# A Strassen-split decoder block on one core: operand pairs for nine Strassen steps per unit, steps prepared in another order, smaller DMA scratch

## The chip, the cores and the metric

The kernel runs on one core of a Trainium2 chip as one program. The metric is the device time of one execution in microseconds; a time of a kernel is the median of several runs. The engines are named as in the profile: PE (TensorE matmul), PEld (its weight load), DVE (VectorE), ACT (ScalarE), POOL (GpSimd) and SP (SyncE, which here only issues loads).

## The reference

A decoder block for 256 tokens of width 4096 in float32. Nearly all of the work is three groups of dense products with 256 rows: the input projection (4096 to 20480 columns), the branch projections (2048 to 4096, twice) and the output projection (4096 to 4096).

```python
def reference(x, norm_w, w_in, pool_w, pool_scale, conv_w, conv_b, gate_b, w_branch, w_out, final_norm_w):
    b, s, d = x.shape
    for l in range(DEPTH):
        h = rmsnorm(x, norm_w[l])
        proj = jnp.einsum('bsd,de->bse', h, w_in[l])
        u_p, z_p, u_c, b_c, c_c, z_c, g_logit = jnp.split(proj, SPLIT_POINTS, axis=-1)
        y_pool = causal_multiscale_pool(u_p, pool_w[l], pool_scale[l]) * jax.nn.silu(z_p)
        y_conv = causal_gated_shortconv(u_c, b_c, c_c, conv_w[l], conv_b[l]) * jax.nn.silu(z_c)
        ys = jnp.stack([y_pool, y_conv], axis=2)
        br = jnp.einsum('bsnc,ncd->bsnd', ys, w_branch[l])
        gates = jax.nn.sigmoid(g_logit.reshape(b, s, N_BRANCHES, d) + gate_b[l])
        merged = jnp.sum(gates * br, axis=2)
        x = x + jnp.einsum('bsd,de->bse', merged, w_out[l])
    return rmsnorm(x, final_norm_w)
```

## The kernel before

**Units and steps.** The columns of every projection are cut into units of 1024. A unit adds up its products over the inner dimension in steps of 256 (two blocks of 128): 16 steps for the input and output units, 8 for the branch units. There are 20 input units (cu, cc, cz, cb for the convolution and pz, pu for the pooling, two of each; eight gate units g0_0 to g1_3), eight branch units b0_0 to b1_3, and four output units o0 to o3, in that order. All their steps together are 448 weight steps, each with 1 MB of weights. Steps of kind B and M, put into the units behind pu0 and pu1, are the pooling's own products.

**Splitting.** Each float32 factor is split into a high and a low part, and a product is three matmuls: high by high, high by low, low by high. ACT copies the high part (a rounded copy), DVE subtracts it from the factor for the low part.

**P and S steps.** A P step (plain) multiplies a 256 x 256 piece of the activations with a 256 x 1024 piece of weights as 2 x 2 x 2 blocks: 8 products, 24 matmuls of 128 x 512, into the four PSUM banks "sums". An S step does the same by a Strassen scheme with seven products, 21 matmuls, into three of these and four banks "shared", which a unit joins with four additions near its end. For that the weights' sums are needed: DVE forms two sums into the tile V, two more in place of the raw weights, and all are split like the rest. The activations' sums (Q3, Q5, Q6, Q7) are stored beside the split operand: an operand of kind P takes 4 KB per partition in the tile `arena`, one of kind S takes 7 (or 9 for the first NB of them, which can also serve as P). There are NP_X = 9 and NS_X = 7 of them; a ninth operand, LATE, is used as S in a few units with its sums kept in DRAM (late_d) and fetched into spare places.

**Which step is S.** Each unit gets a list of kinds: `spread_sequence`, `late_sequence` or `at_places`, which names the places of the S steps outright.

**Preparing.** SP loads weights into `raw`, three buffers in turn; the load of step i + 3 is issued when step i is prepared. A step's preparation is a list of small actions ("micros") with a size and a guard: the size is taken from `ring`, a ring buffer of RING KB per partition that holds split weights, and given back by the matmuls that read it. `pump`, called after every group of matmuls, writes out as many micros as ring, guard and a lookahead of AHEAD = 3 steps allow. This fixes the order of the instructions on every engine; each engine then works in order and waits on semaphores. For an S step the micros are, in this order, `sums` (V), `direct` (ACT's copy of the three direct blocks, 1536 elements, then on DVE a 512 addition, the 1536 subtraction, a 512 addition), `t13` (copy and subtraction of V, 1024) and `t24` (copy and subtraction of the two sums formed in place, 1024).

**Fills and epilogues.** Work beside the main loop is put on a queue, one item per tick; a tick is TICK = 6 matmuls. The first unit's preparation also forms the Strassen sums of x (`x_sums`, `x_parts`, at the steps listed in `seconds`). Sums across tokens' tiles are added by accumulating DMAs from POOL (`move_add`).

Of the kernel before, what the change touches and what calls it, by code (L numbers as in the profile page):

```python
# [26 lines left out]
F32 = mybir.dt.float32  # L27
# [15 lines left out]
NP_X, NS_X = 9, 7  # L43
NB = 1
NP_Y, NS_Y = (6, 5), (2, 3)
RING = 60
# [10 lines left out]
def hybrid_block(ctx: ExitStack, tc: tile.TileContext, x, x_t, norm_t, w_first, w_in, pool_w, pool_scale,  # L57
# [70 lines left out]
    late_d = dram.tile([P, 5, P], F32, name="late_d")  # L128
# [62 lines left out]
    class Operand:  # L191


        def __init__(self, kind, view, region):
            self.kind, self.view, self.region = kind, view, region
            self.ready = False
            self.more = None
            self.more_ready = False

        def block(self, part, i):  # L200

            if self.kind == "S":
                return self.view[:, part, i]
            if i in self.more:
                return self.more[i][:, part]
            return self.view[:, part, {A12: 0, A22: 0, A11: 1, A21: 1}[i], i in (A22, A21)]
# [32 lines left out]

    rg = Ring(RING)  # L240

# [5 lines left out]
    class Step:  # L247
# [7 lines left out]
        def micros(self):  # L255
# [27 lines left out]
            if self.kind == "P":  # L283
                self.blocks, self.h, self.l = [None] * 2, [None] * 2, [None] * 2
                return self.pre + [(8, None, half(0)), (8, None, half(1))] + self.post
            if self.kind == "S":
                q = r.rearrange("p (i n) -> p i n", i=4)
                tv = V

                def sums(_):  # L290
                    add(tv, q[:, 0:1].to_broadcast([P, 2, NH]), q[:, 1:3])

                def direct(block):
# [15 lines left out]
                def t24(block):  # L309
                    self.b24 = block  # L310
                    t = piece(block, 0, 8).rearrange("p (i a n) -> p i a n", i=2, a=2)
                    self.h24, self.l24 = t[:, :, 0], t[:, :, 1]
                    act(self.h24, q[:, 0:2])
                    sub(self.l24, q[:, 0:2], self.h24.bitcast(F32))

                return self.pre + self.post + [(0, None, sums), (12, None, direct), (8, None, t13), (8, None, t24)]
            if self.kind == "B":
                def parts(block):
# [4 lines left out]
                    sub(self.l, R, self.h.bitcast(F32))  # L323

                return [(16, lambda: self.unit.flags.get("base"), parts)]
            if self.kind == "M":
# [4 lines left out]
                def weights(block):  # L331
# [5 lines left out]
                    sub(self.l, q, self.h.bitcast(F32))  # L337

# [265 lines left out]
    LAST_FIRST = ('cc0',)  # L604
    SPREAD = {"cc1":(8,1),"cb1":(8,2),"cu1":{4,5,7,9,10,12,13,15},"cb0":(8,2),"cz0":(7,5),"pz0":{5,7,8,10,11,13,15},"pu0":(7,),"cz1":(7,5),"g1_3":(6,0),"pz1":(7,),"g0_0":(7,),"pu1":{4,6,8,10,12,13,15},"cc0":{2,4,6,8,10,13,15}}
# [26 lines left out]
    def in_unit(name, col, epi, seq=None, **kw):  # L632
        def src(i):
            return win[col // NU, i]
        if name in SPREAD:
            at = SPREAD[name]
            seq = at_places(at) if isinstance(at, set) else spread_sequence(*at)
# [5 lines left out]
        units.append(Unit(name, src, seq or seq_late, x_ops, epi, scaled=True, **kw))  # L643
# [3 lines left out]
    def conv_units(c, first=False):  # L647
# [32 lines left out]
        in_unit(f"cu{c}", base, lambda u: [], seq=seq_0 if first else spread_sequence(NS_X, 4), dst=Y)  # L680
        in_unit(f"cc{c}", base + 2 * HALF, c_epi, seq=seq_even if c else None)
        in_unit(f"cz{c}", base + 3 * HALF, z_epi)
        in_unit(f"cb{c}", base + HALF, b_epi, seq=seq_even)


    def pool_units(c):
# [5 lines left out]
        in_unit(f"pz{c}", HALF + c * NU, z_epi, seq=None if c else seq_turned)  # L692
# [4 lines left out]
    def make_bands(c):  # L697
        nonlocal sa, Y
        if c == 0:
            x_ops[LATE].more_ready = False  # L700

# [78 lines left out]
    def gate_unit(n, c, before=None):  # L780
# [7 lines left out]
        seq = {(0, 0): seq_late, (1, 3): spread_sequence(few)}.get((n, c), seq_even)  # L788
        if (n, c) in ((0,1),(1,1),(0,2),(1,2),(0,3),(1,0),):
            seq = spread_sequence(NS_X + 1, 1 if c else 2)  # L790
# [27 lines left out]

    def out_unit(c):
# [14 lines left out]
        seq = seq_even if c else seq_late  # L834
        if c in (2,):
            seq = spread_sequence(NS_X + 1)
        if c == 1:
            seq = at_places({2,4,6,7,9,11,13,15})

            late_s = [i for k, i in seq if k == 'S']  # L840
            late_s = iter(late_s[1:] + late_s[:1])
            seq = [(k, next(late_s) if k == 'S' else i) for k, i in seq]
        if c == 3:

            seq = spread_sequence(NS_X, 1, TAIL + 0)
        if c == 2:
            seq = at_places({2,4,6,7,9,11,13,15})
# [133 lines left out]
    def insert(u, c, owner):  # L981
# [6 lines left out]
        rest = psteps[5:]  # L988
        while ssteps:
            seq.append(ssteps.pop(0))  # L990
            if rest:
                seq.append(rest.pop(0))
        seq += rest
# [132 lines left out]
    LATE = NP_X - 1  # L1126

    def late_sums():
        o = x_ops[LATE]
        h, l = (o.view[:, part].bitcast(F32) for part in range(2))  # L1130
        q = sa[:, 4:8].rearrange("p (k t) c -> p k t c", t=2)
        add(q, h, l)
        q = q.rearrange("p k t c -> p k (t c)")
        mul(q, q, rbc[:, None].to_broadcast([P, 2, T]))
        sums_s(sa, [sa[:, i] for i in range(4, 8)])
        mul(sa[:, Q3], sa[:, Q3], std)
        move(late_d[:, 0:4], sa[:, 0:4])
        move(late_d[:, 4], sa[:, A11])

    def late_place(pool, o, blocks):  # L1140
        n = len(blocks)
# [433 lines left out]
```

## Time and profile before

| | |
|---|---|
| median of 3 runs | 2378.24 us (2378.23 to 2379.2) |
| profiled execution, first to last instruction | 2376.6 us |
| PE busy | 2364.3 us, 99% |
| DVE busy | 2170.1 us, 91% |
| ACT busy | 1392.8 us, 59% |
| POOL busy | 86.0 us, 4% |
| mean granted TensorE clock | 0.999 |
| 16 DMA engines, mean | 232 GB/s |
| weight loads, issue to landing (w_in) | 4.9 us median |

Busy times of an engine are unions: where two instructions overlap, the time counts once, so a group's busy time can be less than its count times its mean. A matmul's own 390 ns overlaps its neighbours'. An instruction's name "ring<-raw,ring 128x1024" says that it writes the tile ring from raw and ring, 128 partitions by 1024 elements. "L72 DVE" is the helper through which every two-operand vector instruction goes, so line numbers tell little and tile names tell more.

### The profile page before, as it was taken

How to read it: one execution, taken by the hardware profiler on the slowest of the kernel's cores; microseconds unless marked ns; L12 is line 12 of the kernel's file. 1: busy time of each engine (PE TensorE's matmuls, PEld its weight loads, DVE VectorE, ACT ScalarE, POOL GpSimd, SP SyncE). 2: the span in 40 equal slices, each digit the busy share in tenths (PEclk: the TensorE clock that was granted, in tenths of full speed). 3: DMA queues.
4: the chain of work that ended last, by engine and by line, in shares of the span. 5: the costliest groups of instructions: out<-in, count | busy, mean ns of one | idle time of the engine just before them, and what ended most of it. 6: DMA issues, size and time to landing. Idle time of an engine off the chain costs nothing.

```text
span 2376.6 us, 27878 instructions
## 1 busy us (share of the span) xinstructions
PE 2364.3 (99%) x10540; PEld 1957.5 (82%) x10540; DVE 2170.1 (91%) x2195; ACT 1392.8 (59%) x1452; POOL 86.0 (4%) x153
## 2 busy tenths in 40 slices
PE   9999999999999999999999999999999999999998
PEld 7888888888888888888888888888888888888886
DVE  8999999989989978979999999999898898799998
ACT  7565665656546555556655656556664556566554
POOL 0000000000010010000000000000100001000000
PEclk9999999999999999999999999999999999999999
DMA  8464665655665646655776667667766667567666
GB/s 337 161 238 170 235 251 211 217 211 213 212 239 217 238 183 221 231 200 201 259 247 214 235 237 235 228 238 260 263 249 230 226 250 289 209 214 265 241 240 264
DMA packets 83559, 551.25 MB, mean 232 GB/s; under 512 B 9616, under 2 KB 9872, under 8 KB 22240
## 3 DMA queue, kind: packets, MB, share of 16 engines
q1 hardware_dynamic: 68800, 484.51, 54.7%
q0 software_dynamic: 14192, 63.90, 9.6%
q8 instruction: 82, 1.34, 0.2%
q10 hardware_dynamic: 432, 1.07, 0.1%
q14 instruction: 53, 0.43, 0.1%
HBM read 516.60 MB, written 25.49 MB: 228 GB/s over the span
## 4 chain that ended last, share of the span: by engine, by line
PE 98%; DVE 1%; DMA 1%; ACT 0%; SPq 0%; issue 0%; DVEq 0%; ACTq 0%
PE sums L1283 74%; PE shared L1283 21%; PE shared L766 1%; PE shared L509 1%; DMA raw<-in_w_in_dram 0%; DVE R L72 0%; DVE ring L72 0%; DMA raw<-in_w_out_dram 0%; ACT ring L69 0%; PE shared L745 0%; SPq L87 0%; PE shared L746 0%; PE shared L748 0%; SPq L162 0%; ACT V L69 0%
## 5 line engine op out<-in xcount | busy, mean ns | idle before, releaser
L1283 PE MATMUL sums<-ring,arena 128*128 128x512 f32 x7890 | 1858.2, 390 | 0.5 <-ACT arena L69 0.4
L1283 PEld LDWEIGHTS sums<-ring,arena 128*128 128x128 f32 x7890 | 1478.3, 188 | 307.8 <-ACT ring L69 1.2
L69 ACT ACTIVATE ring<-raw 128x1024 fp32r<-128x1024 f32 (+2 forms) x902 | 997.5, 1145 | 703.9 <-DVE raw L72 297.3
L72 DVE TENSOR_TENSOR ring<-raw,ring 128x1024 fp32r<-128x1024 f32 (+2 forms) x902 | 1176.5, 1335 | 142.5 <-ACT ring L69 108.6
L1283 PE MATMUL shared<-ring,arena 128*128 128x512 f32 x2118 | 535.2, 389 | 0.0
L1283 PEld LDWEIGHTS shared<-ring,arena 128*128 128x128 f32 x2118 | 397.6, 188 | 82.5
L69 ACT ACTIVATE ring<-V 128x1024 fp32r<-128x1024 f32 x188 | 198.8, 1058 | 148.3 <-DVE V L72 112.7
L72 DVE TENSOR_TENSOR V<-raw 128x1024 f32<-128x1024 f32 x188 | 229.3, 1220 | 4.7 <-DMA raw<-in_w_in_dram 2.6
L72 DVE TENSOR_TENSOR ring<-V,ring 128x1024 fp32r<-128x1024 f32 x188 | 229.3, 1220 | 0.5 <-ACT ring L69 0.5
L72 DVE TENSOR_TENSOR raw<-raw 128x512 f32<-128x512 f32 x188 | 130.2, 693 | 6.5
L72 DVE TENSOR_TENSOR raw<-V,raw 128x512 f32<-128x512 f32 x188 | 130.0, 692 | 5.8
L72 DVE TENSOR_TENSOR R<-R,E 128x1024 f32<-128x1024 f32 (+1 forms) x49 | 77.5, 1591 | 1.6 <-ACT E L69 0.9
L72 DVE TENSOR_TENSOR R<-R,shared 128x512 f32<-128x512 f32 x87 | 59.5, 684 | 8.9 <-ACT R L69 5.0
L69 ACT ACTIVATE E<-sums,rin 128x512 f32<-128x512 f32 x76 | 50.0, 685 | 15.7 <-PE sums L1283 15.7
L69 ACT ACTIVATE arena<-sa 128x512 fp32r<-128x512 f32 (+2 forms) x42 | 22.4, 559 | 35.5 <-DVE sa L72 35.5
L1283 PE MATMUL shared<-ring,sums 128*128 128x512 f32 x138 | 35.9, 396 | 0.0
L1283 PEld LDWEIGHTS shared<-ring,sums 128*128 128x128 f32 x138 | 25.9, 188 | 6.0
L94 POOL DMA_DIRECT2D R<-E x8 | 7.2, 980 | 513.6 <-ACT ring L69 337.9
L69 ACT ACTIVATE E<-sums 128x512 f32<-128x512 f32 x40 | 22.2, 592 | 5.4 <-PE sums L1283 5.1
L72 DVE TENSOR_TENSOR arena<-sa,arena 128x512 fp32r<-128x512 f32 (+2 forms) x42 | 24.4, 606 | 0.7 <-ACT arena L69 0.7
L94 POOL DMA_DIRECT2D R<-in_gate_b_dram x9 | 10.1, 1119 | 356.0 <-DVE R L72 348.3
L509 PEld LDWEIGHTS shared<-ident,R 128*128 128x128 f32 x160 | 19.4, 140 | 4.2
(149 smaller groups left out, 515.8 us busy)
## 6 DMA issues: line engine op xcount, KB each, us to landing
raw<-in_w_in_dram SPq DMA_DIRECT2D x318, 1024.0 KB, 4.9
raw<-in_w_branch_dram SPq DMA_DIRECT2D x64, 1024.0 KB, 5.4
raw<-in_w_out_dram SPq DMA_DIRECT2D x64, 1024.0 KB, 5.0
gates_d<-R POOLq DMA_DIRECT2D x8, 1024.0 KB, 9.1
R<-in_gate_b_dram POOLq DMA_DIRECT2D x7, 1024.0 KB, 11.2
R<-E POOLq DMA_DIRECT2D x4, 1024.0 KB, 8.7
raw<-in_pool_w_dram SPq DMA_DIRECT2D x4, 1024.0 KB, 5.0
Y<-gates_d POOLq DMA_DIRECT2D x4, 1024.0 KB, 7.9
```

The lines of the kernel that those rows point to most:

```text
L69: return pin(nc.scalar.activation(dst, src, func, **kw))
L72: return pin(nc.vector.tensor_tensor(out=dst, in0=a, in1=b, op=op))
L94: return pin(nc.gpsimd.dma_start(dst, src, accum_op=ALU.add))
L509: pin(nc.tensor.transpose(shared(j)[:, i * T + t * P:i * T + (t + 1) * P], src[:, t, c:c + P], ident))
L766: pin(nc.tensor.matmul(o, a[:, k, ts], b[:, k], start=(k, i) == (0, 0), stop=(k, i) == (3, 2)))
L1283: pin(nc.tensor.matmul(ps, lhs, rhs, start=n == 0, stop=n == u.total[b] - 1))
```

## The change

Four things are changed together.

1. The scratch that is set aside for dynamic DMAs goes from its default, 16384 bytes per partition, to 4096. The 12 KB go to the arena (NP_X, NS_X = 7, 9 and NB = 2: 95 KB for 87) and to the ring (64 KB for 60).
2. With nine stored S operands, the operand LATE with its DRAM copy, its fetches and its spare tiles is gone; two more pairs get their sums in the first units (`seconds`).
3. The S steps' places are written out for each unit: 210 of the 448 steps are S, for 188.
4. The preparation's order: an S step begins with `direct`, which now only issues ACT's copy; then the sums into V, what is held from the step before (`settle`), the 1536 subtraction, and the first 512 addition; `t13`; a place for `t24`; then the head of the next step (its first micro, by `head_of_next`), and only then the second 512 addition and ACT's copy for `t24`. Its subtraction, `low24`, is held and is written out by the next step's `settle`, after that step's first DVE instruction; the raw buffer counts as read only then. P steps put each half's copy and subtraction in separate micros.

```diff
-NP_X, NS_X = 9, 7
-NB = 1
+NP_X, NS_X = 7, 9
+NB = 2
-RING = 60
+RING = 64
...
+    held = []
+
+    def settle():
+
+        while held:
+            held.pop(0)()
...
             if self.kind == "P":
                 self.blocks, self.h, self.l = [None] * 2, [None] * 2, [None] * 2
-                return self.pre + [(8, None, half(0)), (8, None, half(1))] + self.post
+                if self in steps[:2]:
+                    return self.pre + [(8, None, half(0)), (8, None, half(1))] + self.post
...
+                def low(n):
+                    def f(_):
+                        sub(self.l[n], q[:, :, n * NH:(n + 1) * NH], self.h[n].bitcast(F32))
+                        settle()
+                    return f
+                return self.pre + [(8, None, high(0)), (0, None, low(0)), (8, None, high(1)), (0, None, low(1))] + self.post
             if self.kind == "S":
                 q = r.rearrange("p (i n) -> p i n", i=4)
                 tv = V
-
-                def sums(_):
-                    add(tv, q[:, 0:1].to_broadcast([P, 2, NH]), q[:, 1:3])
 
                 def direct(block):
                     self.bd = block
                     d = piece(block, 0, 12).rearrange("p (i a n) -> p i a n", i=3, a=2)
                     self.dh, self.dl = d[:, :, 0], d[:, :, 1]
                     act(self.dh, q[:, 1:4])
+
+                def sums(_):
+                    add(tv, q[:, 0:1].to_broadcast([P, 2, NH]), q[:, 1:3])
+                    settle()
+                    sub(self.dl, q[:, 1:4], self.dh.bitcast(F32))
                     add(q[:, 0], tv[:, 0], q[:, 2])
-                    sub(self.dl, q[:, 1:4], self.dh.bitcast(F32))
-                    add(q[:, 1], q[:, 0], q[:, 3])
...
-                def t24(block):
+                def place24(block):
...
+                def t24(_):
+                    add(q[:, 1], q[:, 0], q[:, 3])
                     act(self.h24, q[:, 0:2])
-                    sub(self.l24, q[:, 0:2], self.h24.bitcast(F32))
-
-                return self.pre + self.post + [(0, None, sums), (12, None, direct), (8, None, t13), (8, None, t24)]
+
+                    def low24():
+                        sub(self.l24, q[:, 0:2], self.h24.bitcast(F32))
+                        self.prepared = True
+                    held.append(low24)
+
+                return self.pre + self.post + [(12, None, direct), (0, None, sums), (8, None, t13), (8, None, place24),
+                                               (0, lambda: head_of_next(self), t24)]
...
+    PLACES = {
+        "cc0": (2, 4, 6, 8, 10, 13, 15),
+        "cz0": (5, 7, 8, 10, 11, 13, 15),
+        "cb0": (3, 5, 6, 8, 9, 11, 12, 14, 15),
+        "cu1": (4, 5, 7, 9, 10, 12, 13, 14, 15),
...
+    GATE = (2, 4, 5, 7, 8, 10, 11, 13, 15)
...
+    OUT = ((5, 7, 8, 10, 11, 13, 15), (2, 4, 6, 7, 9, 11, 12, 13, 15), (2, 4, 6, 7, 9, 11, 13, 15),
+           (1, 3, 4, 6, 7, 9, 10, 12))
...
-    seconds = {14: 10, 15: 11, 16: 12, 17: 13, 19: 14, 21: 15, 28: 9}
+    seconds = {14: 10, 15: 11, 16: 12, 17: 13, 19: 14, 21: 15, 28: 9, 32: 8, 36: 7}
...
-    before(23, late_sums)
-    before(40, early_place)
-    before(41, lambda: early[0]())
-    before(42, lambda: early[1]())
...
+    def head_of_next(s):
+
+        i = state["np"] + 1
+        if i == len(steps):
+            return True
+        t = steps[i]
+        if t.kind not in "PS" or t.pre or t.post and t.kind == "S" or t.started:
+            return True
+        if i <= state["limit"] and t.raw is not None:
+            t.started = micro(t)
+        return t.started or state["np"] <= state["now"] + 1
...
-    nc = _bacc.Bacc("TRN2", target_bir_lowering=False, num_devices=1)
+    nc = _bacc.Bacc("TRN2", target_bir_lowering=False, num_devices=1,
+                     dynamic_dma_scratch_size=4096)
```

More of the change, by code (lines that the diff above doesn't have):

```diff
@@ L603, in hybrid_block @@
     few = NS_X - NB
-    LAST_FIRST = ('cc0',)
-    SPREAD = {"cc1":(8,1),"cb1":(8,2),"cu1":{4,5,7,9,10,12,13,15},"cb0":(8,2),"cz0":(7,5),"pz0":{5,7,8,10,11,13,15},"pu0":(7,),"cz1":(7,5),"g1_3":(6,0),"pz1":(7,),"g0_0":(7,),"pu1":{4,6,8,10,12,13,15},"cc0":{2,4,6,8,10,13,15}}
+    LAST_FIRST = ("cc0",)
+    PLACES = {
[13 rows of a table added]
+    }
+    GATE = (2, 4, 5, 7, 8, 10, 11, 13, 15)
     def late_sequence(ns_):
@@ L833, in src @@
             return wout[c, i]
[L834 to L847, printed above, removed]
+        seq = at_places(OUT[c])
         units.append(Unit(f"o{c}", src, seq, m_ops, epi, before=start))
```

132 lines of the change are left out of this document (48 added, 84 removed), and 9 rows, old and new, of the table PLACES.

## The prediction

> **What bounds the kernel now.** I read the page's engine shares first, then PE's groups, then everything PE ever waited for.
>
> ```profile
> span 2376.6 us, 27878 instructions
> PE 2364.3 (99%) x10540; PEld 1957.5 (82%) x10540; DVE 2170.1 (91%) x2195; ACT 1392.8 (59%) x1452; POOL 86.0 (4%) x153
> PEclk9999999999999999999999999999999999999999
> L1283 PE MATMUL sums<-ring,arena 128*128 128x512 f32 x7890 | 1858.2, 390 | 0.5 <-ACT arena L69 0.4
> L1283 PE MATMUL shared<-ring,arena 128*128 128x512 f32 x2118 | 535.2, 389 | 0.0
> ```
>
> ```profile
> PE shared L1034 <- DVE rout L1039: 1.1, 1, 1.1
> PE sums L1283 <- ACT arena L69: 0.4, 1, 0.4
> ```
>
> PE is busy for 2364.3 of 2376.6 us at the full granted clock, and the second fence is all it waited for: 1.5 us, both at the opening. From the opening to the tail the kernel is one unbroken row of matmuls, and what shortens it is fewer matmuls. What one costs is not its 390 ns, because they overlap; it is their spacing, from the chain of waits (start, length, what):
>
> ```profile
> 1277.36 11.56 PE sums L1283 x51
> 1303.35 6.12 PE sums L1283 x27
> 1359.11 11.56 PE sums L1283 x51
> ```
>
> 27 matmuls in 6.12 us is 0.2267 us each. The first and last of these lines stand at the same place of two neighbouring gate units: a unit of eight S and eight P steps takes 81.75 us. An S step is 7 products of 3 matmuls, 21 x 0.2267 = 4.76 us; a P step is 24, 5.44 us; 8 x 4.76 + 8 x 5.44 = 81.6, so a unit is its steps and next to nothing else.
>
> The second engine is DVE, 91%. It splits weights into high and low parts and forms the S sums. The stretches below are (start:end, length, then PE, PEld, DVE, ACT, POOL): units cu1, a gate unit, and o1.
>
> ```profile
> 342.10:425.70 83.60, 83.60 (x378) 69.17 (x377) 81.35 (x76) 48.03 (x47) 2.01 (x3) 1.00 0.62 225
> 1277.36:1359.11 81.75, 81.75 (x361) 67.60 (x361) 75.78 (x71) 48.48 (x47) 1.77 (x2) 1.00 0.68 232
> 2119.80:2201.50 81.70, 81.70 (x362) 67.58 (x361) 79.03 (x78) 50.68 (x52) 5.15 (x7) 1.00 0.77 264
> ```
>
> DVE has 2.25, 5.97 and 2.67 us left in them. This is the number on which the change turns.
>
> **The change on PE.** The step lists hold 188 S steps of 448 now, and 210 afterwards (91 in the input units for 81, 70 in the gates for 61, 17 in the branches as before, 32 in the output units for 29). Each of 22 steps drops 24 - 21 = 3 matmuls: 66, and the built instruction order has exactly 66 fewer. 66 x 0.2267 = **-14.96 us**, all of it on the bounding engine. Against the profiled span that gives 2376.6 - 15.0 = 2361.6 us, if nothing begins to starve PE.
>
> **What the 22 steps cost DVE.** By form (count | busy, mean ns | idle before):
>
> ```profile
> L72 DVE TENSOR_TENSOR ring<-raw,ring 128x1024 fp32r<-128x1024 f32 x706 | 835.1, 1222 | 104.1 <-ACT ring L69 70.4 <-PE sums L1283 22.5
> L72 DVE TENSOR_TENSOR ring<-raw,ring 128x1536 fp32r<-128x1536 f32 x188 | 329.8, 1754 | 37.0 <-ACT ring L69 36.7
> L72 DVE TENSOR_TENSOR V<-raw 128x1024 f32<-128x1024 f32 x188 | 229.3, 1220 | 4.7 <-DMA raw<-in_w_in_dram 2.6 <-DMA raw<-in_w_out_dram 1.7
> L72 DVE TENSOR_TENSOR ring<-V,ring 128x1024 fp32r<-128x1024 f32 x188 | 229.3, 1220 | 0.5 <-ACT ring L69 0.5
> L72 DVE TENSOR_TENSOR raw<-raw 128x512 f32<-128x512 f32 x188 | 130.2, 693 | 6.5
> L72 DVE TENSOR_TENSOR raw<-V,raw 128x512 f32<-128x512 f32 x188 | 130.0, 692 | 5.8
> ```
>
> An S step is six of these: 1.754 + 1.220 + 1.220 + 1.222 + 0.692 + 0.693 = 6.80 us; a P step is two, 2.44. So each exchange adds 4.36 us, and 22 add 95.9: 2170.1 + 95.9 = 2266.0 us of DVE work in a span of 2361.6, 96%. With the order left as it is this would not do. A gate unit would have 75.78 + 4.36 = 80.1 us of work in 81.75 - 0.68 = 81.07, and 9 S steps that wait for ACT as they do now. How they wait is seen in one step of the DVE timeline (start, length):
>
> ```profile
> 1286.11 1.22 DVE L72 TENSOR_TENSOR ring<-raw,ring 128x1024 fp32r<-128x1024 f32 x1
> 1287.24 1.22 DVE L72 TENSOR_TENSOR V<-raw 128x1024 f32<-128x1024 f32 x1
> 1288.50 0.69 DVE L72 TENSOR_TENSOR raw<-V,raw 128x512 f32<-128x512 f32 x1
> 1289.85 1.76 DVE L72 TENSOR_TENSOR ring<-raw,ring 128x1536 fp32r<-128x1536 f32 x1 [0.66 <-ACT ring L69]
> 1291.64 0.69 DVE L72 TENSOR_TENSOR raw<-raw 128x512 f32<-128x512 f32 x1
> 1292.25 1.22 DVE L72 TENSOR_TENSOR ring<-V,ring 128x1024 fp32r<-128x1024 f32 x1
> 1293.52 3.50 DVE L72 TENSOR_TENSOR ring<-raw,ring 128x1024 fp32r<-128x1024 f32 x3
> 1296.94 1.22 DVE L72 TENSOR_TENSOR V<-raw 128x1024 f32<-128x1024 f32 x1
> ```
>
> Instructions that need nothing of their neighbour start before it ends: 1287.24 - 1286.11 = 1.13 us after a 1024 of 1.22, and (1296.94 - 1293.52)/3 = 1.14. One that needs the result before it starts later: 1288.50 - 1287.24 = 1.26; after the 1536 it is 1.79. The S step as it is takes 1293.52 - 1287.24 + 1.14 = 7.42 us, 0.66 of it the wait for ACT's 1536 copy.
>
> **What the new order gives.** The built order on DVE becomes: sum into V (1024), the previous step's low24 subtraction, the 1536 subtraction, first 512 add, l13 subtraction, second 512 add. ACT's 1536 copy is now issued before the sums, in the head of the step, ahead of the step before it ending. Neither 512 add waits any more for the instruction right in front of it; in the built order both wait for one at least two back. So the spacing is 3 x 1.14 + 1.79 + 2 x 0.61 = **6.43 us** per S step against 6.76 without the wait and 7.42 with it. I keep 1.79 for the 1536 (its own length and a gap), though nothing may hold its follower: if it overlaps as the others do, it is 0.1 less. A P step stays 2.28.
>
> Unit by unit then: 75.78 - 8 x 0.33 + (6.43 - 2.28) = 77.3 us for a gate unit with nine, 3.8 below its 81.07. For cu1, 81.35 - 2.6 + 4.15 = 82.9 in 83.60 - 0.68 = 82.92: nothing left. For o1, 79.03 - 2.6 + 4.15 = 80.6 in 81.02. These two are full, not over, and each has a neighbour with room: cb0 in front of cu1 is the stretch
>
> ```profile
> 260.30:342.10 81.80, 81.80 (x362) 67.62 (x361) 74.91 (x70) 48.88 (x48) 1.45 (x2) 1.00 0.65 232
> ```
>
> and o2 behind o1 keeps its eight. DVE work runs two to three steps ahead of PE (lookahead AHEAD = 3, and the ring now holds 64 KB per partition for 60), some 8 us, so a unit that runs over by one or two takes it from that lead. I put the cost of both at **+0.5 us**, with 0 and 5 as the ends: 5 if both keep 0.3 us of waits per S step (2 x 9 x 0.3).
>
> **Weights' loads.** A raw buffer is given back by low24, which is now held into the next step, behind that step's first instruction; and the step three later is begun before the second 512 add of the step in front.
>
> ```profile
> raw<-in_w_in_dram SPq DMA_DIRECT2D x318, 1024.0 KB, 4.9
> R<-in_gate_b_dram POOLq DMA_DIRECT2D x7, 1024.0 KB, 11.2
> late_d<-sa POOLq DMA_DIRECT2D x1, 256.0 KB, 2.7
> ```
>
> In the order S, P, S, S between the giving back and that head lie one 1024, then 1024 + 1536 + 512 + 1024: 3 x 1.14 + 1.79 + 0.61 = 5.8 us at DVE's own speed; now a P and an S step lie there, 2.28 + 7.42 = 9.7. A load takes 4.9 us, so the margin falls from 4.8 to 0.9 us. SP is the queue that waits, with only other loads behind it; behind a late load stand ACT's head copy, h24, and DVE's next subtraction. It is hidden while loads land in the median time: cost 0 here, and the price if not is a rival.
>
> **The rest.** The two seconds more (x_sums and x_parts at steps 32 and 36, some 3 us of DVE each) replace late_sums and three splits; five POOL transfers with late_d, 2.7 us for the first, go. None of it is on PE's path. POOL is at 4%. With the smaller scratch a transfer could wait for room; the longest, 11.2 us, stands before a gap of 12 ticks of 6 matmuls, 16.3 us, so it may come 5 us later at no cost. I take 0. [...]
>
> **The tail.** DVE and PE end nearly together:
>
> ```profile
> 2343.06 5.77 DVE L72 TENSOR_TENSOR ring<-raw,ring 128x1024 fp32r<-128x1024 f32 x5
> 2350.23 2.36 DVE L72 TENSOR_TENSOR ring<-raw,ring 128x1024 fp32r<-128x1024 f32 x2 [1.40 <-ACT ring L69]
> 2364.10 0.69 DVE L72 TENSOR_TENSOR R<-sums,R 128x512 f32<-128x512 f32 x1
> ```
>
> The last load waits for the last S step's low24, which comes one 1024 later (+1.14) in a step 0.33 to 1 us shorter, after eight S steps that each gained as much. The ends are -0.5 and +1.1; I take **+0.3**.
>
> Sum: -14.96 + 0.5 + 0.3 = -14.2 on the span, 2362.4. The median of the runs shown, 2378.24, is 1.6 above the profiled span, so **2364.0 us**.
>
> **Rivals.**
> *Late loads (0.16).* Loads beside POOL's 1 MB transfers miss the 0.9 us margin. If two per unit land 2 us late, 2 x 1.1 = 2.2 us: the gate units' 3.8 swallow it, cu1 and o1 do not, and and seven more of the units that gain S steps (cb0, cc1, cz1, cb1, pz0, pu0, o3), if as full, pay up to 1 us each: 2.2 x 2 + 7 = 11, 2375. For: the margin shrinks fivefold. Against: POOL's transfers come early in a unit, where P steps are.
> *Slower: low24 stands behind the head on ACT (0.12).* ACT works in order, and the next step's head is put in front of h24, the copy that low24 needs.
>
> ```profile
> 1288.33 1.49 ACT L69 ACTIVATE ring<-raw 128x1536 fp32r<-128x1536 f32 x1 [2.46 <-issue]
> 1289.72 1.05 ACT L69 ACTIVATE ring<-V 128x1024 fp32r<-128x1024 f32 x1
> ```
>
> If the head starts only when the second add is done (for ring space, or its load), low24 waits 1.49 + 1.05 - 1.14 = 1.4 us. A gate unit bears 3.8/9 = 0.42 us per S step, cu1 none; from there it decides. At 0.9 a step (two in three) it costs 9 x 0.9 - 3.8 = 4.3 in each of six gate units and 8 in cu1 and o1: 42, so 2361.6 + 42 + 1.6 = 2405. Against: ACT is at 59%, and ring and lead give it steps of room.
> *No overlap gained (0.03).* If DVE's instructions never overlap, a nine-S unit is 9 x 6.80 + 14 x 1.22 and, for the joins, 4 x 0.684 + 2 x 1.220 from
>
> ```profile
> L72 DVE TENSOR_TENSOR R<-R,shared 128x512 f32<-128x512 f32 x87 | 59.5, 684 | 8.9 <-ACT R L69 5.0 <-PE shared L1283 2.5
> L72 DVE TENSOR_TENSOR R<-R,E 128x1024 f32<-128x1024 f32 x32 | 38.6, 1220 | 0.2
> ```
>
> = 83.4, 2.3 over; in eleven units 25: 2388. The trace speaks against it: the same sum for now's gate unit, 8 x 6.80 + 16 x 1.22 + 5.2 = 79.1, stands above its 75.78. [...]
> *The scratch holds POOL back (0.02).* A second 11.2 us in front of the sigmoid, 22.4 - 16.3 = 6 us in eight gate units: 48, 2411.
>
> **How the numbers follow.** The forecast has 0.67, its own range 2362.5 to 2369. Below it lies only the tail's gain. A change under 0.2%, 4.8 us, counts as none (2373.5 to 2383.0). Late loads split evenly at 2373.5: faster 0.67 + 0.08 = 0.75, the same 0.08, slower 0.12 + 0.03 + 0.02 = 0.17. Leaving out the three slower rivals and a little of the late loads, the range is 2362 to 2376.
>
> **What would show it.** Right: 66 fewer matmuls at an unchanged 0.2267 us; gate units with nine S steps 81.07 us apart; DVE between 93 and 96%; its waits for ACT's ring copies well below what they are; the second 1024 of the pair behind V starting 1.14 us after it. Wrong: any PE wait for DVE in the middle of the run, first in cu1 and o1; ACT waits for raw loads of several us per unit; low24 with an idle ahead of it in most S steps.

## The result and the profile after

| | before | after |
|---|---|---|
| median | 2378.72 us (2378.23 to 2379.31, 4 runs) | 2465.57 us (2463.37 to 2466.66, 4 runs) |
| profiled execution | 2376.6 us | 2463.7 us |
| mean granted clock | 0.999 | 0.990 |

The ratio is 1.0364, 95% interval 1.0349 to 1.0379: 87 us slower, where 14 us faster was forecast. First the page of the changed kernel: its span, the engines, the chain that ended last, PE's two large groups (busy, mean ns, idle before) and the loads (median us from issue to landing).

```profile
span 2463.7 us, 27622 instructions
PE 2391.2 (97%) x10474; PEld 1952.6 (79%) x10474; DVE 2232.3 (91%) x2299; ACT 1420.6 (58%) x1477; POOL 87.0 (4%) x148
PE 51%; DVE 25%; DMA 10%; issue 8%; ACT 6%; ACTq 0%; POOL 0%; DVEq 0%; SPq 0%; POOLq 0%
L1279 PE MATMUL sums<-ring,arena 128*128 128x512 f32 x7596 | 1812.2, 392 | 17.5 <-DVE ring L72 8.4
L1279 PE MATMUL shared<-ring,arena 128*128 128x512 f32 x2520 | 661.2, 396 | 39.5 <-DVE ring L72 28.2
raw<-in_w_in_dram SPq DMA_DIRECT2D x318, 1024.0 KB, 5.1
```

The 66 matmuls are gone (10540 to 10474), but PE's two large groups now stand idle for 57 us where they had 0.5, and half of the chain that ended last is no longer PE: DVE has a quarter of it, loads a tenth. DVE's share of the span is unchanged because the span grew with its work. The view of waits (who waits <- for whom: us in all, count, longest) says where DVE lost its lead:

```profile
ACT ring L69 <- DMA raw<-in_w_in_dram: 166.7, 98, 6.3
DVE ring L72 <- ACT ring L69: 154.7, 125, 6.1
PE shared L1279 <- DVE ring L72: 28.2, 33, 2.8
DVE V L72 <- DMA raw<-in_w_in_dram: 25.2, 13, 3.4
```

and the same rows of the kernel before:

```profile
DVE ring L72 <- ACT ring L69: 114.7, 112, 4.5
ACT ring L69 <- DMA raw<-in_w_in_dram: 24.9, 17, 2.5
DVE V L72 <- DMA raw<-in_w_in_dram: 2.6, 4, 1.2
```

ACT's waits for w_in loads went from 24.9 to 166.7 us; with w_out (8.1 to 41.3) and w_branch (5.7 to 31.7) from 39 to 240. One stall of the changed kernel, in gate unit g0_3 (start, length, what, idle before and its releaser):

```profile
1585.66 1.19 POOL L94 DMA_DIRECT2D R<-in_gate_b_dram  x1 [62.79 <-DVE R L72]
1588.15 22.80 SPq L87 DMA_DIRECT2D raw<-in_w_in_dram  x5
1589.18 1.22 DVE L72 TENSOR_TENSOR V<-raw 128x1024 f32<-128x1024 f32 x1
1590.31 1.75 DVE L72 TENSOR_TENSOR ring<-raw,ring 128x1536 fp32r<-128x1536 f32 x1
1591.98 0.69 DVE L72 TENSOR_TENSOR raw<-V,raw 128x512 f32<-128x512 f32 x1
1592.58 1.22 DVE L72 TENSOR_TENSOR ring<-V,ring 128x1024 fp32r<-128x1024 f32 x1
1593.72 0.68 DVE L72 TENSOR_TENSOR raw<-raw 128x512 f32<-128x512 f32 x1
1596.76 1.23 DVE L72 TENSOR_TENSOR V<-raw 128x1024 f32<-128x1024 f32 x1 [2.35 <-DMA raw<-in_w_in_dram]
1596.77 2.43 ACT L69 ACTIVATE ring<-raw 128x1536 fp32r<-128x1536 f32 x2 [5.20 <-DMA raw<-in_w_in_dram]
1600.51 0.73 PE L1279 MATMUL shared<-ring,arena 128*128 128x512 f32 x2 [0.76 <-DVE ring L72]
1603.78 0.69 DVE L72 TENSOR_TENSOR raw<-raw 128x512 f32<-128x512 f32 x1
1604.58 2.00 ACT L69 ACTIVATE ring<-raw 128x1024 fp32r<-128x1024 f32 x2 [4.43 <-DVE raw L72]
1606.62 2.36 DVE L72 TENSOR_TENSOR ring<-raw,ring 128x1024 fp32r<-128x1024 f32 x2 [2.15 <-ACT ring L69]
1609.04 0.73 PE L1279 MATMUL shared<-ring,arena 128*128 128x512 f32 x2 [2.84 <-DVE ring L72]
```

Lines 3 to 7 are the new order doing what was predicted: starts 1.13, 1.67, 0.60 and 1.14 us apart. The rest is the loss, and there are two kinds of it. At 1596.8 the load is late: two loads were issued 1.1 us apart, just behind POOL's accumulating transfer, and they landed 8.5 and 11.2 us later by the trace. The view of DMAs from 1580 to 1612 us has the median of its five loads:

```profile
raw<-in_w_in_dram SPq DMA_DIRECT2D x5, 1024.0 KB, 8.5
R<-in_gate_b_dram POOLq DMA_DIRECT2D x1, 1024.0 KB, 9.4
```

The head's copy waits for the load on ACT, the copy for t24 stands behind it, low24 waits for that copy, and low24 is what gives the buffer back: by the trace the next loads go out only at 1600.49 and 1609.04. A late load makes the next one late. At 1606.6 there is no load in it: the next step's head had not been begun, so ACT's two copies come only after the second 512 addition and DVE stands still for 2.15 us. Reading the built order, the next P or S step has no head at this point in 22 steps. In 18 of them the ring has no free piece for it; in the other four the program begins no head, because the next step has other work in front of its preparation.

How long units now take, and what follows a PE wait, is seen in the stretches view (start:end, length, PE, PEld, DVE, ACT, POOL, granted clock, DMA share, GB/s): the unit cu1, the unit g0_3, and 3.41 us right after the stall above.

```profile
344.00:431.40 87.40, 83.83 (x374) 68.45 (x373) 82.97 (x79) 48.02 (x46) 2.01 (x3) 1.00 0.59 217
1574.30:1663.00 88.70, 84.36 (x359) 67.79 (x358) 78.66 (x74) 49.59 (x47) 2.35 (x3) 0.98 0.61 217
1609.77:1613.18 3.41, 3.41 (x9) 2.66 (x9) 3.41 (x3) 2.00 (x2) 0.08 (x1) 0.51 1.01 348
```

9 matmuls in 3.41 us, at a granted clock of 0.51. The trace has ten such stretches in mid-run, eight of 3.413 us and two of 6.827, which is 41 us at half speed; before has none outside the tail.

### The profile page after: what moved, and what is told of

Read it like the earlier page. It is cut to its first block, busy times and chain, and to the rows that moved or that the text cites. A ratio compares the mean times of both kernels' runs of the same rounds, so it can differ in the third digit from the quotient of the medians.

```text
span 2463.7 us, 27622 instructions
## 1 busy us (share of the span) xinstructions
PE 2391.2 (97%) x10474; PEld 1952.6 (79%) x10474; DVE 2232.3 (91%) x2299; ACT 1420.6 (58%) x1477; POOL 87.0 (4%) x148
## 4 chain that ended last, share of the span: by engine, by line
PE 51%; DVE 25%; DMA 10%; issue 8%; ACT 6%; ACTq 0%; POOL 0%; DVEq 0%; SPq 0%; POOLq 0%
PE sums L1279 39%; DVE ring L72 14%; PE shared L1279 10%; DMA raw<-in_w_in_dram 8%; ACT ring L69 5%; DVE raw L72 4%; DVE R L72 3%; DVE V L72 2%; DMA raw<-in_w_out_dram 1%; PE shared L804 1%; PE shared L535 1%; DMA raw<-in_w_branch_dram 1%; DVE arena L72 1%; DMA sa<-y_d 0%; ACT R L69 0%
## 5 line engine op out<-in xcount | busy, mean ns | idle before, releaser
L1279 PE MATMUL sums<-ring,arena 128*128 128x512 f32 x7596 | 1812.2, 392 | 17.5 <-DVE ring L72 8.4
L1279 PEld LDWEIGHTS sums<-ring,arena 128*128 128x128 f32 x7596 | 1428.9, 189 | 323.9 <-DVE ring L72 13.8
L1279 PE MATMUL shared<-ring,arena 128*128 128x512 f32 x2520 | 661.2, 396 | 39.5 <-DVE ring L72 28.2
L1279 PEld LDWEIGHTS shared<-ring,arena 128*128 128x128 f32 x2520 | 474.8, 190 | 161.2 <-DVE ring L72 45.6
L69 ACT ACTIVATE ring<-V 128x1024 fp32r<-128x1024 f32 x210 | 222.2, 1058 | 194.3 <-DVE V L72 174.1
L72 DVE TENSOR_TENSOR V<-raw 128x1024 f32<-128x1024 f32 x210 | 256.3, 1221 | 32.2 <-DMA raw<-in_w_in_dram 25.2
L72 DVE TENSOR_TENSOR ring<-V,ring 128x1024 fp32r<-128x1024 f32 x210 | 256.0, 1219 | 0.7 <-ACT ring L69 0.7
L72 DVE TENSOR_TENSOR raw<-V,raw 128x512 f32<-128x512 f32 x210 | 144.0, 686 | 0.0
L535 PE MATMUL shared<-ident,R 128*128 128x128 f32 x160 | 23.0, 273 | 1.7 <-DVE R L72 1.6
L804 PE MATMUL shared<-ring 128*128 128x512 f32 x96 | 22.1, 389 | 0.0
```

Of the source, the lines that this page charges most:

```text
L69: return pin(nc.scalar.activation(dst, src, func, **kw))
L72: return pin(nc.vector.tensor_tensor(out=dst, in0=a, in1=b, op=op))
L535: pin(nc.tensor.transpose(shared(j)[:, i * T + t * P:i * T + (t + 1) * P], src[:, t, c:c + P], ident))
L804: pin(nc.tensor.matmul(o, a[:, k, ts], b[:, k], start=(k, i) == (0, 0), stop=(k, i) == (3, 2)))
L1279: pin(nc.tensor.matmul(ps, lhs, rhs, start=n == 0, stop=n == u.total[b] - 1))
```

## The experiments

Three causes were set against each other. LATE LOADS: raw is given back too late. MISSED HEADS, with the ring's space as what decides: the next step's head can't be begun. VECTORE FULL: units of nine S steps with other work in them don't fit DVE at all. PE's own work without a stall puts 210 S steps at 2378.4 - 14.96 = 2363.4 us; each kernel's "floor" below is 2378.4 less 0.68 us (3 x 0.2267) for each S step over 188. The kernel before took 2377.87 to 2379.31 us in all comparisons. Each time below is that of one execution, except for the last two kernels, which ran ten times each within 3.6 us.

**The parts of the change, one by one.** New order and stored operands, S steps at places much like before (190); then 210 S steps in the order of before; then the smaller scratch alone on the kernel before.

```diff
-    GATE = (2, 4, 5, 7, 8, 10, 11, 13, 15)
+    GATE = (1, 3, 5, 7, 8, 10, 12, 14)
```

> The changed kernel with its order of preparation, operands, ring and scratch, but the S steps at the places of the kernel before (190 instead of 210; 188 before). Theory LOADS (the new order gives a raw buffer back later and begins the step three later sooner, so loads land late and ACT, DVE and then PE wait): still slower than before, 2400 to 2440 us, ACT's waits for raw loads over 100 us against 39 before. Theory DVE FULL (22 more S steps are more than DVE can do, the order is innocent): 2372 to 2380 us, raw-load waits near 40 us.

```diff
-                return self.pre + self.post + [(12, None, direct), (0, None, sums), (8, None, t13), (8, None, place24),
-                                               (0, lambda: head_of_next(self), t24)]
+                return self.pre + self.post + [(0, None, sums), (12, None, direct), (8, None, t13), (8, None, t24)]
```

> The changed kernel with 210 S steps, nine S operands, ring of 64 and small scratch, but the micros of P and S steps in the order of the kernel before (sums, direct with both additions, t13, t24 with its subtraction at once; nothing held, no head ahead). LOADS: faster than the changed kernel, 2390 to 2440 us, waits for raw loads back under 80 us, waits of DVE for ACT at the 1536 subtraction as before (0.66 us in each S step). DVE FULL: at least as slow as the changed kernel, 2465 us or more, because DVE's work is the same and its spacing worse.

```diff
+                     dynamic_dma_scratch_size=4096)
```

> The kernel before with the scratch for dynamic DMAs at 4096 bytes and nothing else. LOADS and DVE FULL: no change, 2377 to 2380 us. SCRATCH HOLDS POOL BACK: 2400 us and more, POOL's transfers issued or landing later.

Measured: 2402.38 us (floor 2377.0), 2407.81 (floor 2363.4) and 2378.09. The scratch costs nothing. The new order loses 25 us even without the added steps, and its waits for loads are those of the changed kernel (165.1 us for w_in); with 210 steps in the old order they are gone:

```profile
ACT ring L69 <- DMA raw<-in_w_in_dram: 18.6, 21, 2.1
PE sums L1270 <- DVE ring L72: 10.5, 15, 1.4
```

So the order that was to make room is the dearer half: 58 of the 102 us between the changed kernel and its floor are not there without it.

**The new order's two devices.** Taken out of it one at a time: t24 no longer waits for the next head; low24 follows at once instead of being held.

```diff
-                                               (0, lambda: head_of_next(self), t24)]
+                                               (0, None, t24)]
```

> The changed kernel without the head ahead: the second 512 addition and h24 are written out without first beginning the next step; low24 is still held. LOADS with the coupling on ACT (h24 stuck behind a head that waits for its load): 2400 to 2440 us, low24's idle near 0, raw-load waits clearly below 240 us. LOADS by the late giving back alone: 2450 to 2465 us. DVE FULL: 2465 us.

```diff
-                    held.append(low24)
+                    low24()
```

> The changed kernel with low24 written out right behind h24 instead of being held into the next step; the head is still ahead. The raw buffer is free one 1024 instruction (1.14 us) sooner, but low24 stands behind h24 and the head on ACT. LOADS by the late giving back: 2420 to 2450 us. LOADS by the coupling on ACT: 2465 us or slower, with idle ahead of low24 of 1 us and more in many S steps. DVE FULL: 2465 us or slower.

2691.8 and 2604.81 us. The first is far above all that was expected of it, the second is as the coupling on ACT had it. Within this order each device is needed; without the heads DVE pays the ACT copies at step after step:

```profile
DVE ring L72 <- ACT ring L69: 354.1, 207, 6.1
PE shared L1279 <- DVE ring L72: 119.4, 76, 4.0
```

That is the price of a missed head, multiplied.

**Loads.** First halved, so that they are late less often (the second half of each weight load is left out from the seventh load on, so these steps multiply stale weights).

```diff
+        elif i < 6:
             load(r.rearrange("p (k n) -> p k n", k=2), s.src)
+        else:
+            load(r.rearrange("p (k n) -> p k n", k=2)[:, 0:1], s.src[:, 0:1])
```

> The changed kernel, but from the seventh weight load on only the first half of each raw buffer is loaded (the other half keeps the weights of an early load, so the products use wrong weights; no instruction on PE, DVE or ACT changes). Loads are half as long. LOADS: ACT's waits for raw loads fall from 240 to under 60 us and the time to 2390 to 2425 us. RING AND HEAD (22 S steps for whose follower no head could be begun in time, and DVE's fullness): 2440 us or more although the loads' waits are gone.

2426.73 us, 39 less. This doesn't take lateness away altogether: a half load still takes 3.9 us in the median, and ACT's waits for w_in, w_out and w_branch fall to 97 us (73.6 for w_in), where under 60 was expected. Then with real loads and an earlier giving back: the two 512 sums go to a tile of their own, W, so that raw is free at the second 512 addition and not at low24. W takes 4 KB, so a ring of 60 with and without it:

```diff
-                    add(q[:, 1], q[:, 0], q[:, 3])
-                    act(self.h24, q[:, 0:2])
+                    add(W[:, 1], W[:, 0], q[:, 3])
+                    self.read = True
+                    act(self.h24, W)
...
-            if nl < len(loaded) and (nl < NRAW or loaded[nl - NRAW].prepared):
+            if nl < len(loaded) and (nl < NRAW or loaded[nl - NRAW].prepared or loaded[nl - NRAW].read):
```

> The changed kernel with one thing moved: the two sums that were formed in place of the raw weights go to a tile W of their own (4 KB, for which the ring gives up 4 KB, 60 for 64), so a raw buffer is given back by the second 512 addition and no longer by the held low24, two to three us sooner. Everything else, order and places, stays. LOADS (late giving back makes the loads late): waits of ACT for raw loads fall from 240 to under 100 us and the time to 2380 to 2420 us. If the held low24 or ACT's order is the cause and the loads only follow: loads' waits fall but the time stays above 2440 us.

> The changed kernel with the ring at 60 and nothing else: the control of the run before. LOADS: within 15 us of the changed kernel, 2455 to 2480 us, loads' waits near 240 us. If ring space is what binds: well above 2480 us.

2523.65 and 2588.9 us. W takes 65 us off; but 4 KB less ring alone had cost 123, where LOADS had expected less than 15, so the first of the two missed its 2380 to 2420 by far. In the built order the steps without a head go from 22 to 77, which is what the ring's last 4 KB were for. A fourth raw buffer, paid for with a ring of 56, tells the same:

```diff
-RING = 64
-NRAW = 3
+RING = 56
+NRAW = 4
```

> The changed kernel with four raw buffers for three (8 KB, taken from the ring: 56 for 64). A load may now start one whole step sooner. LOADS: waits for raw loads under 60 us and 2380 to 2420 us, unless the smaller ring takes some of it back. RING SPACE: slower than 2465 us.

2556.59 us: loads are hardly waited for, 116 steps have no head. The same pair where W fits beside a ring of 64, with eight stored S operands and 197 S steps (floor 2372.3), late and early giving back:

```diff
-NP_X, NS_X = 7, 9
-NB = 2
+NP_X, NS_X = 8, 8
+NB = 1
```

> The changed kernel's order, ring of 64 and small scratch, with eight S operands (NP_X, NS_X, NB = 8, 8, 1) and every unit of nine S steps at eight: 197 S steps, 39 matmuls more than with 210. Control of the next run. LOADS: between the 2402 us of the order with 190 S steps and 2465, some 2415 to 2440, with raw-load waits of 200 us and more. RING AND HEAD: 2400 to 2420 (10 followers without a head for 22).

> The same 197 S steps with the two sums in a tile W of their own, so that a raw buffer is given back by the second 512 addition instead of by low24; the ring stays at 64 here. This isolates the giving back. PE's floor is 2376.6 - 27 x 0.2267 = 2370.5 of span, 2372 us. LOADS: raw-load waits under 60 us and 2372 to 2392 us. RING AND HEAD: within 10 us of the control.

2416.41 and 2393.08 us (the second 1 us above what LOADS expected), waits for w_in loads 163 and 39.7 us. And the first experiment's 190 steps, with W and that operand split:

> The 190 S steps at the places of before, the new order, and the tile W: against the 2402 us of the order alone. LOADS: 2375 to 2382 us, PE nearly without waits. RING AND HEAD: 2395 us or more.

2381.32 us for 2402.38. Giving back late is worth 21 to 65 us in three pairs (the last of them also differs in the operand split), and 39 come back when loads are halved. W and the earlier giving back were always put in together; that it is the loads that gain is read from their waits. LATE LOADS is one cause. That it isn't the only one is not shown by the halved loads, with 97 us of waits left, but by the smaller rings above and the runs that follow.

**Heads, alone and with the loads.** head_of_next lets t24 go without a head when the step is next in line; here only when it is itself to be multiplied. Then 4 steps have no head in place of 22.

```diff
-        return t.started or state["np"] <= state["now"] + 1
+        return t.started or state["np"] <= state["now"]
```

> The changed kernel with one comparison altered: t24 of a step may go before the next step's head only when the step is already the one to be multiplied (np <= now), not one step earlier. By the order in which the program issues its pieces, 22 steps go without a next head in the changed kernel and 4 here; nothing else moves, and the lead at which low24 comes is the same. MISSED HEADS (a share of the loss is the 2.16 us that VectorE waits at each step without a head, and what TensorE then waits behind it, half clock included): 18 such stalls fewer, 2.2 us each of VectorE, 2465.6 goes to 2425 to 2450. LATE LOADS alone: the raw-load waits of ScalarE stay near 240 us and the time within 5 us of 2465.6. VECTORE FULL (it can't recover a lead that is lost, wherever it was lost): 2455 to 2475, since t24 now waits longer for the head.

> The loads halved as in the earlier run of the changed kernel with half loads (2426.73), and the comparison np <= now besides: loads and missed heads are both out of the way, VectorE's work is that of the changed kernel. LATE LOADS plus MISSED HEADS as the two causes: 2370 to 2395, near the 2363.7 that TensorE's own work would give. VECTORE FULL (nine S steps of sixteen leave it no room to recover a lead): 2415 or more, with PE still waiting for VectorE in the gate units of nine S steps.

> The changed kernel whole (nine S steps to a gate unit, 210 S steps), with the three remedies together: the sums of S11 and S22's 512 columns go to a tile W, so that raw is given back at the second 512 addition; the comparison np <= now; a ring of 63, with 1024 of scratch so that W fits. The earlier run with W at a ring of 60 and 77 missed heads took 2523.65; here 4 heads are missed. LATE LOADS plus MISSED HEADS: raw-load waits of ScalarE below 60 us, time 2375 to 2410. RING (the lead itself lacks space, whatever the heads do): 2440 to 2530. VECTORE FULL: 2420 or more with raw-load waits below 60.

2444.26, 2411.56 and 2407.45 us. Heads are worth 21 us alone and 15 beside halved loads; that second run lies between its two expectations, with 92 us of waits for loads left. In the third, with W and every load whole, these waits are 49.5 us in all (before: 39). So with both causes mended at 210 S steps, 58 of the 102 us are back; 44 are not. Of that last kernel, three stretches: a gate unit of nine S steps, cu1, and o0.

```profile
1303.80:1384.70 80.90, 80.90 (x359) 67.01 (x358) 78.55 (x75) 49.90 (x48) 1.77 (x2) 1.00 0.68 235
344.10:431.70 87.60, 85.02 (x375) 69.69 (x374) 83.33 (x80) 50.03 (x49) 2.00 (x3) 0.98 0.62 224
2055.20:2145.60 90.40, 87.11 (x381) 70.14 (x380) 83.51 (x107) 53.21 (x64) 2.14 (x4) 0.98 0.54 191
```

The gate unit runs at PE's pace with nine S steps and DVE at 78.55 of 80.90. cu1 and o0 have over 83 us of DVE work in units that PE could do in 82.9 and 84.1. From the first matmul of each unit to that of the next, in us; the floor is the length before, less 0.68 for each S step added:

| unit | before | floor at 210 | after | 210, old order | 210, both mended | 195, both mended |
|---|---|---|---|---|---|---|
| cu1 | 83.6 | 82.9 | 87.4 | 87.0 | 87.6 | 83.5 |
| cz1 | 84.2 | 83.5 | 90.2 | 86.6 | 86.1 | 84.3 |
| pz0 | 84.2 | 83.5 | 86.5 | 86.9 | 89.9 | 84.2 |
| pz1 | 98.8 | 97.4 | 105.8 | 101.0 | 102.7 | 98.1 |
| g0_0 | 98.8 | 97.4 | 102.9 | 100.5 | 103.9 | 98.1 |
| g1_0 to g0_3, six units | 490.5 | 486.4 | 516.9 | 492.8 | 486.5 | 489.6 |
| o0 | 84.8 | 84.1 | 91.3 | 87.7 | 90.4 | 87.6 |
| o1 to o3 | 244.1 | 242.8 | 264.6 | 249.5 | 247.7 | 243.9 |

The two remedies mend the gate units (30 us) and o1 to o3 (17). What stays, 32 us in cu1, cz1, pz0, pz1, g0_0 and o0 alone, is in units where DVE has fills or epilogues to do beside the steps, and 21 us of it are there in the old order too. By a unit's total, DVE's work is more than PE's only in cu1; g0_0 and pz1 seem to have 6 us of room (DVE 91.2 and 91.6 us for 97.4). But DVE's gaps lie early in the unit. The 40 us that end at the longest PE wait of pz1 and of g0_0, in the same kernel:

```profile
909.80:949.80 40.00, 37.16 (x160) 29.25 (x159) 39.90 (x39) 23.21 (x22) 0.00 (x0) 1.00 0.52 186
1095.42:1135.42 40.00, 37.17 (x161) 29.62 (x159) 39.90 (x39) 23.10 (x22) 0.00 (x0) 1.00 0.54 188
```

DVE is busy for 39.90 of 40 us. The same stretch has 39.88 in pz0, 39.95 in cz1 and 37.84 in cu1, which is over by its total. That is VECTORE FULL in these five units, over their last stretch and not over the whole unit. o0 is another case: DVE is busy for 35.59 of the 40 us, and what ends the wait is ACT.

```profile
2117.60 1.04 ACT L69 ACTIVATE ring<-V 128x1024 fp32r<-128x1024 f32 x1
2118.67 1.23 DVE L72 TENSOR_TENSOR ring<-V,ring 128x1024 fp32r<-128x1024 f32 x1 [2.15 <-ACT ring L69]
```

V was ready at 2112.1, but its copy stands on ACT behind three copies that split a stored operand, and those waited until 2116.56 for DVE's sums of that operand. The groups of DVE in that unit (count | busy, mean ns | idle before) have more of these splits than before the change. Before:

```profile
L72 DVE TENSOR_TENSOR arena<-sa,arena 128x512 fp32r<-128x512 f32 x6 | 4.0, 686 | 0.7 <-ACT arena L69 0.7
```

and after, where there are two further S operands to store:

```profile
L72 DVE TENSOR_TENSOR arena<-sa,arena 128x512 fp32r<-128x512 f32 x9 | 6.0, 686 | 2.1 <-ACT arena L69 2.1
```

**A version with fewer S steps.** Eight stored operands, W, early giving back, 195 S steps: one S step fewer in pz0 and in o3 than the run of 197, and the seven of o0 spread otherwise; then the same with the altered comparison. (The first text counts from 190 S steps; the kernel before has 188, so it is 7 steps, 21 matmuls, 4.8 us, and the floor is 2373.6.)

```diff
-        "pz0": (5, 7, 8, 10, 11, 13, 14, 15),
+        "pz0": (5, 7, 8, 10, 11, 13, 15),
```

> 195 S steps: eight operands of each kind, W and the early giving back as in the run of 197 (2393.08), and in pz0, o0 and o3, where that run lost 9, 9 and 2 us, one S step fewer and the places spread. 5 S steps more than before are 16.5 matmuls fewer, 3.7 us: with no stall 2374. LATE LOADS plus MISSED HEADS: 2373 to 2380, raw-load waits below 60 us, one S step without a head. If what is left of the loss hangs on the sum of VectorE's work rather than on these places: 2385 or more.

> The 195 S steps of the run before (2383.91), with t24 waiting for the next head until its own step is the one to be multiplied (np <= now). In that run VectorE waited 2.15 us, and TensorE 1.8 to 1.9 us behind it, near 816 and 994 us, where a P step of pu0 and one of pu1 had no head. MISSED HEADS: these two gaps go and nothing comes in their place: 2379 to 2381. If t24's longer wait costs the lead elsewhere: 2383 or more.

2383.91 us (ratio 1.0025, 95% interval 1.0015 to 1.0034) and 2377.85 us (0.9999, 0.9989 to 1.0008). The first lies between its two expectations, the second is 1 us better than expected. In the first, near 816 us, a P step without a head:

```profile
814.55 1.06 ACT L69 ACTIVATE ring<-W 128x1024 fp32r<-128x1024 f32 x1 [4.19 <-DVE W L72]
816.59 1.23 DVE L72 TENSOR_TENSOR ring<-raw,ring 128x1024 fp32r<-128x1024 f32 x1 [2.15 <-ACT ring L69]
819.01 0.73 PE L1281 MATMUL shared<-ring,arena 128*128 128x512 f32 x2 [1.84 <-DVE ring L72]
```

and the same place in the second, where nothing waits:

```profile
814.45 0.68 DVE L72 TENSOR_TENSOR W<-W,raw 128x512 f32<-128x512 f32 x1
815.05 1.22 DVE L72 TENSOR_TENSOR ring<-raw,ring 128x1024 fp32r<-128x1024 f32 x1
816.32 1.22 DVE L72 TENSOR_TENSOR ring<-W,ring 128x1024 fp32r<-128x1024 f32 x1
```

The best version found is no faster than the kernel before: 4.8 us of matmuls are saved and 4.2 of stalls, 3.5 of them in o0, take them back. Whether six S steps in o0 would end these is not shown.

## Why the prediction was wrong

**Right.** 66 matmuls at 0.2267 us; the spacing of the S step on DVE, predicted 6.43 us, is 1.13 + 1.67 + 0.60 + 1.14 and, by the trace's other starts, 0.60 and 1.14 more, 6.28; a gate unit with nine S steps does fit DVE, 78.55 us for the predicted 77.3, and runs at 80.90 us for 81.07 once loads and heads are in time. The rival by which DVE never overlaps falls with the same starts: 1.13 us between starts of instructions of 1.22. The scratch is free, as said: 2378.09.

**Wrong: "Weights' loads ... cost 0 here".** This is the step that failed first. The margin of 0.9 us was worked out rightly, and then set against the median landing. The median of the w_in loads held (5.1 us for 4.9; those of w_branch and w_out rose from 5.4 and 5.0 to 6.7 and 6.2), but a margin is eaten by the loads above the median. The trace of before could have said so: 87 of its 318 w_in loads took more than the 5.8 us that the new order leaves. Then two buffers given back 1.1 us apart send two loads at once, beside POOL's transfer, and these landed in 8.5 and 11.2 us. The other half of the error is that the chain was taken as open: "behind a late load stand ACT's head copy, h24, and DVE's next subtraction" names what waits, but not that the last of it, low24, gives back the next buffer. In a closed loop lateness stays. Hence 240 us of waits and 21 to 65 us of time, where the rival *Late loads* had two loads per unit late by 2 us and 11 us of time.

**Wrong: "ring and lead give it steps of room".** The rival in which low24 stands behind the head had the right engine and the wrong event. What costs is not a head in front of h24, 1.4 us, but a head that isn't there: up to 2.15 us of DVE each time, and PE stalls behind it. With 18 more heads begun in time, 21 us came back. The lead of "some 8 us" was read from AHEAD = 3 and the ring's 64 KB. Every step with heads and held parts keeps more of the ring for longer, and 64 was just enough for most steps, not room: 60 cost 123 us more.

**Wrong in size, and by the most: "+0.5 us" for the full units.** 44 us are left when loads and heads are mended, some 25 of them in five full units and 6 in o0. cu1 was predicted to need 82.9 us and has 83.33 when all else is mended, so DVE's work was sized well. But a unit with nothing left isn't carried by its neighbour's lead: it takes 87.6 us where its floor is 82.9, near the 5 that was the upper end for cu1 and o1 together. And the list of full units was too short: o0, pz0, cz1, pz1 and g0_0 were not gone through one by one as cu1 was (o1 itself takes 81.1 once mended), and a unit's total would not have shown pz1 and g0_0, where DVE has no gap in the last 40 us. The work for the two further operands was counted in the first units, "some 3 us of DVE each" off PE's path, and not in o0, where such splits delay ACT's copy of V.

**How the three add.** 102.2 us from 2363.4 to 2465.6: 21 by heads, 37 more by W and early giving back, 44 left. The order of taking them matters (halved loads first: 39, then 15).

**Not settled.** How much of this is the half clock. By an estimate from the ten slow stretches, 41 us at half the clock are 20 us of matmuls not done, but DVE works on meanwhile (3.41 of 3.41 us in both stretches shown). Stalls cost much without it, too: the run of 210 steps in the old order is 44 us above its floor with a single slow stretch of 3.413 us in mid-run. Nor were the 44 us at 210 steps taken apart by runs of their own: that 32 of them lie in these six units is read from the table, and that fewer S steps take most of it away, outside o0, is shown at 195. Why DVE could not work further ahead in the early part of pz1 and g0_0, where it had gaps, is open.

## What to carry to other kernels

Where one instruction's end gives back the buffer from which that same chain is fed, set the margin against the slowest loads of a busy stretch (here 8.5 and 11.2 us), not against the median (5.1), and ask whether a late load makes the next one late. A lead on an engine that was planned at 96% was not earned back here (cu1: 87.6 us for a floor of 82.9): go through every unit's work, its last stretch as well as its total, and give the saving step only to units with room, since in cu1 the ninth S step saved 0.68 us on PE and cost about 4. Ring space that looks spare may be what lets the next step begin; count, in the built order, the steps that begin too late.

## What was not expected of the hardware

PE ran at half the clock for 3.41 us after two waits of under 1 us each. In the changed kernel, PE's own timeline (idle before in brackets) and the stretch behind it:

```profile
1256.40 0.49 PE L1279 MATMUL shared<-ring,arena 128*128 128x512 f32 x1 [0.87 <-ACT ring L69]
1257.66 0.83 PE L1279 MATMUL shared<-ring,arena 128*128 128x512 f32 x2 [0.77 <-DVE ring L72]
1258.29 1.48 PE L1279 MATMUL sums<-ring,arena 128*128 128x512 f32 x3
```

```profile
1258.00:1261.41 3.41, 3.41 (x10) 2.63 (x9) 3.41 (x4) 0.24 (x1) 0.00 (x0) 0.52 0.74 274
```

Two waits of 0.87 and 0.77 us were followed by 3.41 us at a clock of 0.52, ten matmuls in place of fifteen. This trace's slow stretches of mid-run are 3.413 us long or twice that, and 1.64 us of idle in two pieces went ahead of this one. When the changed kernel's trace is cut into pieces of 3.413 us, along the starts of its slow stretches, these go with the idle time of PE in the piece before. After seven full-speed pieces with 2.06 to 2.92 us of it, the next ran at half the clock every time; after four with 1.64 to 1.71 us, three times; after any other full-speed piece of mid-run, none with more than 1.44 us, never. Once the clock was down, 0.77 and 1.41 us of idle were followed by a second slow piece. The wait of 1.84 us at 819.01 us in the first version of 195 steps was not followed by a slow stretch; by an estimate that counts the same 3.413 us back from its one slow stretch, at the end, that wait falls into two pieces, with about 1.0 and 0.8 us. So in the changed kernel a stall of 1.64 us cost, by an estimate, 1.1 us (the five matmuls, at 0.2267) to 1.6 us (3.413 us at the granted clock of 0.52) of PE's time beside itself.
